# A hybrid encoder on one core: the attention core with scores over 128 rows and fewer, wider value products

## The chip, the cores and the metric

The kernel runs on one core of a Trainium2 chip. Its engines are PE (TensorE, matrix products, with its own weight loads), DVE (VectorE), ACT (ScalarE), POOL (GpSimd) and SP (SyncE, which here issues the DMAs). Matmul results land in PSUM, which has eight banks of 128 partitions by 512 float32 numbers; everything else stays in SBUF. The metric is the device time of one execution in microseconds, as a median of several runs.

## The reference

The program is an encoder of two layers on x of 512 positions and 1024 features, in float32. Cut to what matters, a layer computes:

```
h = rmsnorm(x); proj = h @ w_in        # 2304 columns: group A q, k, v and group B q, k, v
qa, ka, qb, kb = rope(rmsnorm per head of 64)
# group A: 8 query heads, 2 kv heads, dim 64, window of +-128, a sink logit per head
p = exp(s - m) / (sum exp(s - m) + exp(sink - m));   ya = p @ va
# group B: 4 heads, two score maps each (c = 0, 1), value dim 128
w = softmax(s[0]) - lam * softmax(s[1]);             yb = rmsnorm(w @ vb) * (1 - lam_init)
x = x + concat(ya, yb) @ w_out
h = rmsnorm(x); gate, val = split(h @ w_up)          # 2 x 2816 columns
x = x + (silu(dwconv3(gate)) * val) @ w_down
```

## The kernel before

**Precision.** A float32 operand is held as two float32r parts: high (the rounded value, written by ACT) and low (what is left, a subtraction on DVE). A product is the sum of three matmuls, high times high, high times low and low times high (`mm3`, L193 to L196). `split_out` (L245 to L247) makes the two parts of a result in PSUM. `emit_unit` does the same for the weights, which stream in over one DMA queue, three units ahead of their use.

**Stages of a layer.** Both the input projection of group A (`akv`, then `aq0`, `aq1`) and the feed-forward run as plain loops. Between them stands a weave of two tracks. One, `attend`, does group A in 8 units (a pair of query-head positions `ip` and a block of 128 queries `qb`) and then group B in 16 units (half, `qb`, head `j`). The other is a chain: the projections of B's first and second half (`proj_b`), the output projection in two passes, and the first half of its last part. `weave` takes the next step from the track that has used the smaller share of its budget (`ATT` 92.0 against 98.6), by the costs that the steps yield. `out_pass(0)` waits for group A's output, `out_pass(1)` for half 0 of B, B's half for its keys.

**Order.** The text of the program gives each instruction a priority, and a scheduler in the build puts the instructions of every engine into a fixed order; an instruction whose buffer is not free in its reckoning is passed by others. A tile of a pool goes into any free buffer of its tag. The matmuls on PE therefore do not stand in the order of the text.

**Queries and keys** (`qk_out`). A projected block of 128 positions is scaled, normed per head (the query's norm is kept apart in `rqa`, `rqb` and applied in the exponent), rotated by POOL and DVE, transposed by PE in the bank `tq`, and split into high and low, with two heads of 64 on the 128 partitions. The columns are permuted so that the two heads of one transposed block of A belong to kv heads 0 and 1.

**Scores.** `a_scores` (L399) and `b_scores` (L488) contract 64 rows: the heads, or the two maps c, lie in the two halves of the partitions. Each score tile takes three matmuls of 64 rows (L412 and L502). Then follow the row maximum on DVE, the exponent on ACT with the row's sum, and scaling or mixing on DVE.

**Values.** `a_values` (L445) transposes the probabilities of four heads in a key block into a bank of 512 columns, splits them, and multiplies them by A's values of both kv heads at once, three products of 512 columns a block. Of each kv head's product only the half of the partitions that belongs to it is kept. `b_values` (L520) transposes the mixed probabilities and adds up twelve products of 128 columns in half of the bank `acc`. `b_norm` (L544) norms, transposes and splits the result.

**Buffers.** `pair` (8) and `keep` (10) hold tiles of 128 x 2 x 512: split queries and keys, A's keys and values, B's values, the attention outputs, and in the feed-forward the hidden tiles `act`. `tmp` (7) holds scores and probabilities, `prob` (6) the transposed parts, `rp` (7) the projected blocks at work. Of PSUM, `mm` has 2 banks, `at` 4, `acc` 1 and `tq` 1.

Of the kernel before, what the change touches and what calls it, by code (L numbers as in the profile page):

```python
# [16 lines left out]
P = 128  # L17
S = 512
# [12 lines left out]
ATT = 92.0  # L31
AHEAD = 3
LAG = 2
RP = 7
# [9 lines left out]
def kernel(  # L44
# [23 lines left out]
    def pair(name):  # L68
        return sb.tile([P, 2, S], F32R, tag="pair", bufs=8, name=name)

    def keep(name):
        return sb.tile([P, 2, S], F32R, tag="keep", bufs=10, name=name)
# [4 lines left out]
    def prob(name):  # L77
        return sb.tile([P, S], F32R, tag="prob", bufs=6, name=name)

    def tmp(name, n=S):  # L80
        return sb.tile([P, n], F32, tag="tmp", bufs=7, name=name)
# [185 lines left out]
    for l in range(depth):  # L267
        lam_init = 0.8 - 0.6 * math.exp(-0.3 * l)
# [55 lines left out]
        def qk_out(bank, t, n, tab, dst, nm, rq):  # L324
            nh = n // HD
            nm = f"{nm}{l}_{t}"
            if n == P:
                raw = bank
            else:
                raw = rp(f"raw_{nm}")  # L330
                nc.scalar.activation(raw, bank[:, :n], AF.Copy, scale=r_tok[:, t:t + 1])
# [21 lines left out]
            nc.gpsimd.tensor_tensor(out=raw, in0=raw, in1=tb, op=ALU.add)  # L353
            tr = tq(f"tr_{nm}")
            nb = n // P
            for b in range(nb):
                nc.tensor.transpose(tr[:, b * P:(b + 1) * P], raw[:, b * P:(b + 1) * P], ident)
            split_out(dst[0][:, :, t * P:(t + 1) * P] if nb > 1 else dst[0][:, t * P:(t + 1) * P],
                      dst[1][:, :, t * P:(t + 1) * P] if nb > 1 else dst[1][:, t * P:(t + 1) * P],
                      tr[:, :n].rearrange("p (b q) -> p b q", q=P) if nb > 1 else tr[:, :n])  # L360
# [5 lines left out]

        # group A keys and values, then queries
        ka_t, va_t = keep(f"ka{l}"), keep(f"va{l}")
        ka = (ka_t[:, 0], ka_t[:, 1])
        va = (va_t[:, 0], va_t[:, 1])  # L370

        def akv_done(bank, t):
            raw = rp(f"raw_kv{l}_{t}")
            nc.scalar.activation(raw, bank[:, :CW], AF.Copy, scale=r_tok[:, t:t + 1])
            split_out(va[0][:, t * P:(t + 1) * P], va[1][:, t * P:(t + 1) * P], raw[:, P:])
            qk_out(raw[:, :P], t, P, tabs[1], ka, "ka", None)
# [4 lines left out]
        qa = [(pair(f"qah{l}_{i}"), pair(f"qal{l}_{i}")) for i in range(2)]  # L381

        def proj_a(i, alloc):
            yield from project(f"aq{i}", lambda bank, t: qk_out(
                bank, t, CW, tabs[0], qa[i], f"qa{i}", rqa[:, t, 2 * i:2 * i + 2, :].rearrange("p a b -> p (a b)")), alloc)
# [8 lines left out]
        ya = [(keep(f"yh{l}_{i}"), keep(f"yl{l}_{i}")) for i in range(2)]  # L394
# [4 lines left out]
        def a_scores(ip, qb):  # L399
# [3 lines left out]
            nm = f"a{l}_{ip}_{qb}"  # L403
            q, k = qa[ip], ka
            mx = small(f"mx_{nm}", 4)
            so = []
            for i in range(2):
                sc = [at(f"sc_{nm}_{i}_{g}") for g in range(2)]
                for j, (u, v) in enumerate(((0, 0), (0, 1), (1, 0))):
                    for g in range(2):  # L410
                        rs = slice(g * HD, (g + 1) * HD)
                        nc.tensor.matmul(sc[g][:, :n], lhsT=q[u][rs, i, qb * P:(qb + 1) * P],  # L412
                                         rhs=k[v][rs, kb0 * P:kb1 * P], start=j == 0, stop=j == 2)
                for g in range(2):
                    s = tmp(f"so_{nm}_{i}_{g}")
                    nc.vector.tensor_tensor_reduce(out=s[:, :n], in0=sc[g][:, :n], in1=mask_sb[:, m0:m0 + n],
                                                   op0=ALU.add, op1=ALU.max, scale=1.0, scalar=-3.0e38,
                                                   accum_out=mx[:, 2 * i + g:2 * i + g + 1])
                    so.append(s)
                yield 1.0  # L420
            by_g = lambda v: v.rearrange("p (g i) -> p i g", g=2)[:, 2 * ip:2 * ip + 2, :]
            pairs = lambda v: v.rearrange("p (i g) -> p i g", g=2)
            rq = rqa[:, qb, 2 * ip:2 * ip + 2, :]
            ngm = small(f"ng_{nm}", 4)
            nc.vector.tensor_tensor(out=pairs(mx), in0=pairs(mx), in1=rq, op=ALU.mult)
            nc.vector.scalar_tensor_tensor(out=pairs(ngm), in0=pairs(mx), scalar=-1.0, in1=by_g(nsink),
                                           op0=ALU.mult, op1=ALU.min)
            dn = small(f"dn_{nm}", 4)
            nc.vector.tensor_tensor(out=pairs(dn), in0=pairs(ngm), in1=by_g(sink), op=ALU.add)
# [3 lines left out]
            for i in range(4):  # L433
                nc.scalar.activation(so[i][:, :n], so[i][:, :n], AF.Exp, bias=ngm[:, i:i + 1],
                                     scale=rqa[:, qb, 2 * ip + i // 2, i % 2:i % 2 + 1],
# [52 lines left out]
        def b_scores(half, qb, j):  # L488
            h = 2 * half + j
            if j == 0:  # L490
                b_st[half, qb] = small(f"bl{l}_{half}_{qb}", 4)
# [304 lines left out]
```

## Time and profile before

| what | value |
|---|---|
| median of 3 runs | 1301.93 us (1301.84 to 1304.04) |
| span of the profiled execution | 1302.4 us |
| PE busy | 1270.6 us, 98% of the span |
| PE weight loads busy | 1056.6 us, 81% |
| DVE busy | 772.9 us, 59% |
| ACT busy | 557.5 us, 43% |
| POOL busy | 385.4 us, 30% |
| HBM read | 99.73 MB, 78 GB/s over the span |

| stage | from, to (us) |
|---|---|
| layer 0: first norm, projection of A | 0, 55 |
| layer 0: attention weave | 55, 285 |
| layer 0: end of output projection, norm, feed-forward | 285, 645 |
| layer 1: projection of A | 645, 691 |
| layer 1: attention weave | 691, 923 |
| layer 1: the rest | 923, 1302 |

The profile shows one execution. A line of groups names the program line, the engine, the operation, what it writes and reads, the shape and the count; behind the bar stand the busy time, the mean duration in ns, and the idle time ahead of it with what ended it. Lines in helpers (L194 to L196, L246, L247) serve many places, so the tile's name tells them apart. Matmuls overlap: the start of the next one, and not the duration, tells what one costs.

### The profile page before, as it was taken

How to read it: one execution, taken by the hardware profiler on the slowest of the kernel's cores; microseconds unless marked ns; L12 is line 12 of the kernel's file. 1: busy time of each engine (PE TensorE's matmuls, PEld its weight loads, DVE VectorE, ACT ScalarE, POOL GpSimd, SP SyncE). 2: the span in 40 equal slices, each digit the busy share in tenths (PEclk: the TensorE clock that was granted, in tenths of full speed). 3: DMA queues.
4: the chain of work that ended last, by engine and by line, in shares of the span. 5: the costliest groups of instructions: out<-in, count | busy, mean ns of one | idle time of the engine just before them, and what ended most of it. 6: DMA issues, size and time to landing. Idle time of an engine off the chain costs nothing. (4 is left out here: it accounts for less than half of the span.)

```text
span 1302.4 us, 17571 instructions
## 1 busy us (share of the span) xinstructions
PE 1270.6 (98%) x6744; PEld 1056.6 (81%) x6744; DVE 772.9 (59%) x1425; ACT 557.5 (43%) x1027; POOL 385.4 (30%) x446
## 2 busy tenths in 40 slices
PE   6999899999999999999999999999899999999998
PEld 6988788687888888888899878877788888888887
DVE  7678787767655324554466786767765543355532
ACT  4566555435433223333455656544443332233321
POOL 6847376114211000110156654741411110011100
PEclk8999999999999999999999999999999999999999
DMA  5211112113332233332331211111133322433232
GB/s 181 91 33 49 58 33 65 33 33 97 98 97 85 85 106 97 98 97 79 100 98 66 65 33 33 56 59 33 33 113 97 97 81 94 117 98 98 79 106 90
DMA packets 32628, 102.96 MB, mean 79 GB/s; under 512 B 3616, under 2 KB 4000, under 8 KB 32544
## 3 DMA queue, kind: packets, MB, share of 16 engines
q1 hardware_dynamic: 32544, 101.84, 25.6%
q8 instruction: 53, 0.87, 0.3%
q14 instruction: 31, 0.25, 0.1%
HBM read 99.73 MB, written 2.10 MB: 78 GB/s over the span
## 5 line engine op out<-in xcount | busy, mean ns | idle before, releaser
L181 ACT CAST wh<-wr 128x1024 fp32r<-128x1024 f32 (+3 forms) x210 | 197.7, 944 | 400.1 <-PE up L195 192.0
L195 PE MATMUL up<-nf_l,wh 128*128 128x512 f32 x704 | 275.3, 391 | 2.3 <-DVE nf_l L213 1.9
L196 PE MATMUL up<-nf_h,wl 128*128 128x512 f32 x704 | 274.5, 390 | 1.2 <-DVE wl L182 0.9
L194 PE MATMUL up<-nf_h,wh 128*128 128x512 f32 x704 | 272.9, 390 | 0.0
L182 DVE TENSOR_TENSOR wl<-wr,wh 128x1024 fp32r<-128x1024 f32 (+3 forms) x174 | 193.3, 1114 | 112.2 <-ACT wh L181 111.8
L702 POOL TENSOR_TENSOR cv<-cv,rb 128x512 f32<-128x512 f32 x44 | 57.8, 1316 | 521.5 <-ACT cv L701 521.5
L195 PEld LDWEIGHTS up<-nf_l,wh 128*128 128x128 f32 x704 | 132.1, 188 | 33.6 <-DVE nf_l L213 6.6
L196 PEld LDWEIGHTS up<-nf_h,wl 128*128 128x128 f32 x704 | 132.1, 188 | 29.7 <-DVE wl L182 2.9
L194 PEld LDWEIGHTS up<-nf_h,wh 128*128 128x128 f32 x704 | 132.2, 188 | 27.6
L195 PE MATMUL dn<-act,wh 128*128 128x512 f32 x352 | 138.5, 394 | 0.0
L196 PE MATMUL dn<-act,wl 128*128 128x512 f32 x352 | 138.4, 394 | 0.0
L194 PE MATMUL dn<-act,wh 128*128 128x512 f32 x352 | 137.9, 393 | 0.0
L182 POOL TENSOR_TENSOR wl<-wr,wh 128x1024 fp32r<-128x1024 f32 x36 | 87.1, 2421 | 89.4 <-ACT wh L181 89.4
L695 DVE TENSOR_TENSOR gp<-up,rb 128x512 f32<-128x512 f32 x44 | 30.3, 693 | 103.4 <-PE up L196 101.8
L703 DVE TENSOR_TENSOR cv<-cv,up 128x512 f32<-128x512 f32 x44 | 30.2, 687 | 82.6 <-POOL cv L702 73.0
L194 PEld LDWEIGHTS dn<-act,wh 128*128 128x128 f32 x352 | 66.0, 188 | 16.0
L195 PEld LDWEIGHTS dn<-act,wh 128*128 128x128 f32 x352 | 66.0, 187 | 15.7
L196 PEld LDWEIGHTS dn<-act,wl 128*128 128x128 f32 x352 | 66.0, 188 | 15.4
L716 DVE TENSOR_TENSOR x<-x,dn 128x512 f32<-128x512 f32 x32 | 22.0, 689 | 78.4 <-PE dn L196 78.4
L509 ACT ACTIVATE e_b<-sc_b,mx_b,rqb 128x512 f32<-128x512 f32 x64 | 49.2, 774 | 38.6 <-DVE mx_b L506 38.6
L701 ACT ACTIVATE cv<-cv 128x512 f32<-128x512 f32 x44 | 27.8, 632 | 76.4 <-DVE cv L700 76.3
L505 DVE TENSOR_REDUCE mx_b<-sc_b 128x1 f32<-128x512 f32 x64 | 42.0, 681 | 0.2
(211 smaller groups left out, 2713.7 us busy)
## 6 DMA issues: line engine op xcount, KB each, us to landing
wr<-w_up SPq DMA_DIRECT2D x88, 512.0 KB, 3.6
wr<-w_in SPq DMA_DIRECT2D x36, 512.0 KB, 3.7
wr<-w_down SPq DMA_DIRECT2D x32, 384.0 KB, 3.1
wr<-w_down SPq DMA_DIRECT2D x32, 320.0 KB, 2.9
wr<-w_out SPq DMA_DIRECT2D x16, 512.0 KB, 3.6
x<-xT SPq DMA_DIRECT2D x8, 256.0 KB, 5.3
outT<-x SPq DMA_DIRECT2D x8, 256.0 KB, 2.0
rows<-row_par SPq DMA_DIRECT2D x2, 260.0 KB, 5.0
```

Of the source, the lines that this page charges most:

```text
L181: nc.scalar.copy(hi[:, o], raw[:, o])
L182: eng.tensor_tensor(out=lo[:, o], in0=raw[:, o], in1=hi[:, o], op=ALU.subtract)
L194: nc.tensor.matmul(acc, lhsT=a[0], rhs=b[0], start=start, stop=False)
L195: nc.tensor.matmul(acc, lhsT=a[0], rhs=b[1], start=False, stop=False)
L196: nc.tensor.matmul(acc, lhsT=a[1], rhs=b[0], start=False, stop=stop)
L505: nc.vector.tensor_reduce(out=mx[:, c:c + 1], in_=sc[c], axis=AX, op=ALU.max)
L509: nc.scalar.activation(e[c], sc[c], AF.Exp, bias=mx[:, c:c + 1], scale=rq[:, c:c + 1], accum_out=lsum[:, 2 * j + c:2 * j + c + 1])
L695: nc.vector.tensor_tensor(out=g[:, 1:S + 1], in0=acc[0], in1=rb, op=ALU.mult)
L701: nc.scalar.activation(cv, cv, AF.Silu)
L702: nc.gpsimd.tensor_tensor(out=cv, in0=cv, in1=rb, op=ALU.mult)
L703: nc.vector.tensor_tensor(out=cv, in0=cv, in1=acc[1], op=ALU.mult)
L716: nc.vector.tensor_tensor(out=x_sb[d], in0=x_sb[d], in1=acc, op=ALU.add)
```

## The change

- **Keys** are written twice by POOL before the transpose (`k_twice`), so that each head's 64 rows stand on both halves of the partitions, once as high and once as low parts. Their tiles are of 128 x 4 x 512 (`kset`, 4 buffers).
- **Queries** stay as float32 rows until a block is needed. `q_stack`, now in the attention track, transposes it and stacks the high part of a head on one half of the partitions and the low part on the other.
- **Scores** then take two matmuls of 128 rows each: the stack against the doubled high keys, and against the doubled low keys. This adds the product of the two low parts.
- **Values of A**: a unit is now a kv head `g` and a block of queries, with its four heads. The stationary operand holds the kv head's high values in one half of the columns and its low values in the other; two products of 512 columns a block, one for each part of the probabilities. The two halves of the result are added afterwards, through a tile `rd`. Products follow the transposes one block behind.
- **Values of B**: the high parts of the probabilities meet high and low values side by side, 256 columns at once, and the low parts the high values, 128 columns. `acc` holds both results, and `b_norm` adds them.
- **Buffers**: one pool `blk` (10) and `kset` (4) stand in place of `pair` and `keep`; `rd` (2) and `qd` (3) are new; `tmp` has 6, `prob` 4, `rp` 4.
- **Weave**: budgets 73.0 and 107.0, and smaller costs for the attention's steps.

The diff, cut to its core:

```diff
-ATT = 92.0
+ATT = 73.0
+REST = 107.0
-RP = 7
+RP = 4
...
+    def blk(name, dtype=F32R):
+        return sb.tile([P, 2, S], dtype, tag="blk", bufs=10, name=name)
+    def kset(name):
+        return sb.tile([P, 4, S], F32R, tag="kk", bufs=4, name=name)
...
-            nc.gpsimd.tensor_tensor(out=raw, in0=raw, in1=tb, op=ALU.add)
+            if twice is None:
+                nc.gpsimd.tensor_tensor(out=raw, in0=raw, in1=tb, op=ALU.add)
+            else:
+                both = lambda v: v.rearrange("p (h d) -> p h d", d=HD).unsqueeze(2).broadcast_to([P, nh, 2, HD])
+                nc.gpsimd.tensor_tensor(out=twice.rearrange("p (h u d) -> p h u d", u=2, d=HD), in0=both(raw),
+                                        in1=both(tb), op=ALU.add)
+        def k_twice(bank, t, raw, tab, nm, hi, lo):
+            nh = raw.shape[1] // HD
+            tw = rd(f"tw_{nm}{l}_{t}")[:, :nh * P]
+            normed(bank, t, raw, tab, nm, None, tw)
+            tr = tq(f"tr_{nm}{l}_{t}")
+            for h in range(nh):
+                nc.tensor.transpose(tr[:, h * P:(h + 1) * P], tw[:, h * P:(h + 1) * P], ident)
+            split_out(hi[:, :, t * P:(t + 1) * P], lo[:, :, t * P:(t + 1) * P],
+                      tr[:, :nh * P].rearrange("p (h q) -> p h q", q=P))
+        def q_stack(pairs, nm):
+            tr = tq(f"tr_{nm}")
+            for i, q in enumerate(pairs):
+                nc.tensor.transpose(tr[:, i * P:(i + 1) * P], q, ident)
+            trv = tr[:, :2 * P].rearrange("p (i q) -> p i q", q=P)
+            st = qd(f"q_{nm}").rearrange("p (i c q) -> p i c q", c=2, q=P)
+            for c in range(2):
+                a, o = slice(c * HD, (c + 1) * HD), slice((1 - c) * HD, (2 - c) * HD)
+                nc.scalar.copy(st[a, :, c], trv[a])
+                nc.vector.tensor_tensor(out=st[o, :, c], in0=trv[a], in1=st[a, :, c], op=ALU.subtract)
+            return st
...
+            for i in range(4):
+                sc = at(f"sc_{nm}_{i}")
+                for u in range(2):
+                    nc.tensor.matmul(sc[:, :n], lhsT=a_q[qb][i // 2][:, i % 2, g], rhs=ka[:, 2 * u + g, kb0 * P:kb1 * P],
+                                     start=u == 0, stop=u == 1)
...
+            def product(b):
+                v = va[:, kb0 + b, 2 * g:2 * g + 2, :].rearrange("p x e -> p (x e)")
+                for u in range(2):
+                    nc.tensor.matmul(pv, lhsT=v, rhs=pb[b][u], start=b + u == 0, stop=b + u == nkb)
...
+            rs, ro = slice(g * HD, (g + 1) * HD), slice((1 - g) * HD, (2 - g) * HD)
+            y = rd(f"y_{nm}")
+            nc.scalar.copy(y[rs, :S], pv[ro])
+            nc.vector.tensor_tensor(out=y[rs, :S], in0=pv[rs], in1=y[rs, :S], op=ALU.add)
...
-            for i, (u, v) in enumerate(((0, 0), (0, 1), (1, 0))):
-                for c in range(2):
-                    rs = slice(c * HD, (c + 1) * HD)
-                    nc.tensor.matmul(sc[c], lhsT=q[u][rs, j, qb * P:(qb + 1) * P], rhs=k[v][rs, j, :],
-                                     start=i == 0, stop=i == 2)
+            for c in range(2):
+                for u in range(2):
+                    nc.tensor.matmul(sc[c], lhsT=b_st[half, qb, "q"][:, j, c], rhs=k[u][:, 2 * j + c, :],
+                                     start=u == 0, stop=u == 1)
...
+            for w, u in ((wh, 2), (wl, 1)):
+                for b in range(NT):
+                    v = vb[half, b // 2][:, b % 2, j, :u, :].rearrange("p u e -> p (u e)")
+                    nc.tensor.matmul(yb[:, 2 * j * P:(2 * j + u) * P], lhsT=w[:, b * P:(b + 1) * P], rhs=v,
+                                     start=u == 2 and b == 0, stop=u == 1 and b == NT - 1)
...
-            nc.scalar.copy(y, yb)
+            nc.scalar.copy(yv, yb[:, :, 0, :])
+            nc.vector.tensor_tensor(out=yv, in0=yb[:, :, 1, :], in1=yv, op=ALU.add)
...
-              (chain(proj_b(0), proj_b(1), out_pass(0, mm), out_pass(1, mm), out_tail()), 98.6))
+              (chain(proj_b(0), proj_b(1), out_pass(0, mm), out_pass(1, mm), out_tail()), REST))
...
-                a = (pair if f % 2 else keep)(f"act{l}_{f}")
+                if f - f0 < 10:
+                    a = blk(f"act{l}_{f}")
+                elif f - f0 == 10:
+                    last_act = kset(f"act{l}_{f}")
+                    a = last_act[:, 0:2]
+                else:
+                    a = last_act[:, 2:4]
```

More of the change, by code (lines that the diff above doesn't have):

```diff
@@ L77, in prob @@
     def prob(name):
[L78 removed]
+        return sb.tile([P, S], F32R, tag="prob", bufs=4, name=name)
     def tmp(name, n=S):
[L81 removed]
+        return sb.tile([P, n], F32, tag="tmp", bufs=6, name=name)
     def rp(name):
```

160 lines of the change are left out of this document (68 added, 92 removed).

## The prediction

> **What bounds the kernel now.** I read the page first, then the busy time of the engines stage by stage, the order of instructions on TensorE inside the stage that is changed, the groups of VectorE instructions, and the waits.
>
> ```profile
> PE 1270.6 (98%) x6744; PEld 1056.6 (81%) x6744; DVE 772.9 (59%) x1425; ACT 557.5 (43%) x1027; POOL 385.4 (30%) x446
> PE   6999899999999999999999999999899999999998
> DVE  7678787767655324554466786767765543355532
> PE 27%; DVE 0%; issue 0%
> ```
>
> TensorE (PE) is busy almost throughout, and what the chain of waits names is matmuls. But a matmul's busy time overlaps its successor's, so a busy PE says only that it is fed. VectorE (DVE) is busy in seven to eight tenths of slices 1 to 10 and 21 to 29: the two attention stages. The change lies almost wholly in these, and the stage table puts them at 55 to 285 us and 691 to 923 us:
>
> ```profile
> 120.00:130.00 10.00, 10.00 (x72) 8.72 (x71) 9.41 (x22) 7.31 (x19) 8.36 (x9) 1.00 0.18 53
> 130.00:140.00 10.00, 9.25 (x69) 8.15 (x68) 9.39 (x23) 3.64 (x10) 5.02 (x5) 1.00 0.18 54
> ...
> 55.00:285.00 230.00, 222.73 (x1418) 183.15 (x1418) 175.71 (x430) 125.56 (x300) 117.18 (x114) 0.99 0.15 48
> 691.00:923.00 232.00, 226.78 (x1464) 189.51 (x1462) 168.42 (x433) 127.50 (x301) 112.11 (x103) 0.99 0.16 47
> ```
>
> The columns after the length are PE, weight loads, DVE, ACT and POOL. PE fills 97% and 98% of the stages, DVE 76% and 73%. The first two rows are the densest DVE stretch that I found: 94% over 20 us, with PE at 96%. So PE bounds these stages, and DVE is the next engine, not far behind.
>
> **What a matmul costs here** is the distance from one start to the next. Three pieces of the PE's order of time (start, duration) give the prices:
>
> ```profile
> 148.53 0.28 PE L196 MATMUL pj_bq<-wh,na_l 128*128 128x256 f32 x1
> 148.66 0.28 PE L194 MATMUL pj_bq<-wh,na_h 128*128 128x256 f32 x1
> 148.86 0.49 PE L502 MATMUL sc_b<-bkh,bqh 64*128 64x512 f32 x1
> 149.20 0.39 PE L502 MATMUL sc_b<-bkl,bqh 64*128 64x512 f32 x1
> 149.43 0.39 PE L502 MATMUL sc_b<-bkh,bql 64*128 64x512 f32 x1
> 149.76 0.50 PE L194 MATMUL pv_a<-ph_a,va 128*128 128x512 f32 x1
> ...
> 863.31 0.50 PE L502 MATMUL sc_b<-bkl,bqh 64*128 64x512 f32 x2
> 863.64 0.40 PE L502 MATMUL sc_b<-bkh,bql 64*128 64x512 f32 x2
> 863.87 0.39 PE L502 MATMUL sc_b<-bkl,bqh 64*128 64x512 f32 x1
> 864.11 0.39 PE L502 MATMUL sc_b<-bkh,bql 64*128 64x512 f32 x1
> 864.43 0.33 PE L538 MATMUL yb<-vb,wth_b 128*128 128x128 f32 x1
> ```
>
> ```profile
> 255.28 0.27 PE L538 MATMUL yb<-vb,wth_b 128*128 128x128 f32 x1
> 255.39 0.28 PE L539 MATMUL yb<-vb,wth_b 128*128 128x128 f32 x1
> ...
> 125.19 0.33 PE L412 MATMUL sc_a<-ka,qah 64*128 64x384 f32 x1
> 125.36 0.33 PE L412 MATMUL sc_a<-ka,qal 64*128 64x384 f32 x1
> ...
> 126.19 0.39 PE L196 MATMUL pv_a<-ph_a,va 128*128 128x512 f32 x1
> 126.42 0.39 PE L194 MATMUL pv_a<-ph_a,va 128*128 128x512 f32 x1
> ...
> 119.09 0.60 PE L457 MATMUL pt_a<-ident,so_a 128*128 128x128 f32 x4
> 119.62 0.44 PE L412 MATMUL sc_a<-ka,qah 64*128 64x384 f32 x1
> ```
>
> 512 moving columns cost 0.23 us, 384 0.17, 256 about 0.12 (148.53 to 148.66), 128 0.11, a transpose 0.13. So halving a 256-column product into two of 128 nearly doubles its price. Three score matmuls of 64 rows take 0.90 us, not 3 x 0.23: 0.1 is lost when PE goes from 128 rows to 64, and 0.1 when it goes back. Where six of both halves stand together they take 1.12 us: two of them start together, so halves of the array do work side by side there.
>
> The Trainium skill, "TensorEngine Tiling (Array Packing)", under Overview and Key Properties, says that a contraction of at most 64 rows can run as two independent tiles, up to twice as fast, and that changing the tiling mode drains TensorE. That speaks against this change: by the first half of it six old score matmuls would cost 3 x 0.23 = 0.70 us and the four new ones 0.93, so the scores would get dearer, the gains of 25.5 and 18.8 us below would turn into losses of some 7 and 5, and of their sum about 5 us would be left. The trace agrees with the drain (0.1 us each way) and only in part with the overlap: most runs are threes of one half, because the order on PE has separated the halves.
>
> **The change on PE**, both layers together. The busy time of the two kinds of scores, as a tile's rows over the whole span (PE is the first column after the length; scores of B, then of A):
>
> ```profile
> 0.00:1302.40 1302.40, 54.85 (x192) 26.91 (x192) 42.02 (x64) 52.10 (x128) 0.99 0.26 79
> ...
> 0.00:1302.40 1302.40, 37.35 (x192) 23.12 (x192) 29.85 (x64) 0.99 0.26 79
> ```
>
> - Scores of B: 192 matmuls of 64 rows become 128 of 128 rows. 54.9 us goes to 128 x 0.23 = 29.4. Gain 25.5. Bounds: had all stood as sixes, 32 x (1.12 + 0.1) = 39 us, gain 9.6; all as threes, 64 x 1.0 = 64, gain 34.6. The row lies between and is taken.
> - Scores of A: 192 become 128, half of 384 and half of 256 columns: 37.4 goes to 64 x 0.17 + 64 x 0.12 = 18.6. Gain 18.8.
> - Values of A: 120 products of 512 columns become 80 (the stationary operand holds high and low values of one kv head, so one product does for two). Gain 40 x 0.23 = 9.2.
> - Values of B: 384 of 128 columns, 42.2 us, become 128 of 256 and 128 of 128: 15.4 + 14.1 = 29.5. Gain 12.7.
> - Transposes: keys are written twice side by side, so 32 more for B and 8 more for A: 40 x 0.13 = 5.2 lost. The query transposes move from the projection to the attention track, the same number.
>
> Sum on PE: 25.5 + 18.8 + 9.2 + 12.7 - 5.2 = 61.0 us, 30.5 a layer. The stages would last 199.5 and 201.5 us if PE alone set them.
>
> **The change on DVE and its neighbours.** Rows for the operations that multiply (busy, mean ns):
>
> ```profile
> L247 DVE TENSOR_TENSOR pl_a<-pt_a,ph_a 128x512 fp32r<-128x512 f32 x40 | 27.0, 684 | 6.1 <-ACT ph_a L246 6.0
> L247 DVE TENSOR_TENSOR yl<-pv_a,yh 64x256 fp32r<-64x256 f32 x32 | 13.4, 419 | 2.3 <-ACT yh L246 1.8
> L247 DVE TENSOR_TENSOR bkl<-tr_bk,bkh 128x256 fp32r<-128x256 f32 x16 | 6.6, 414 | 2.2 <-ACT bkh L246 2.2
> ...
> L246 ACT CAST ph_a<-pt_a 128x512 fp32r<-128x512 f32 x40 | 22.1, 586 | 14.3 <-PE pt_a L457 13.8
> L246 ACT CAST yh<-pv_a 64x256 fp32r<-64x256 f32 x32 | 11.7, 366 | 36.4 <-DVE yl L247 18.7 <-PE pv_a L196 17.5
> ...
> L702 POOL TENSOR_TENSOR cv<-cv,rb 128x512 f32<-128x512 f32 x44 | 57.8, 1316 | 521.5 <-ACT cv L701 521.5
> L353 POOL TENSOR_TENSOR raw_bk<-raw_bk,sq_bk 128x256 f32<-128x256 f32 x16 | 12.1, 758 | 1.0
> ```
>
> Fewer partitions buy nothing (64x256 costs what 128x256 does). Stacking a query block takes two subtractions of 64 partitions in place of one of 128: 32 stacks, 32 more at 0.42 = 13.4 us. B's key split widens from 256 to 512: 16 x 0.27 = 4.3; A's from 128 to 256, 8 x 0.13 = 1.0. A's two half sums must be added: 16 x 0.68 = 10.9. B's too: 16 x 0.42 = 6.7. Together 36.3 us, 18.2 a layer, none taken away. ACT gets 32 x 0.37 + 16 x 0.59 + 16 x 0.22 + 1 = 26 us, 13 a layer: 126 becomes 139 of some 215 us, so it hides behind PE and DVE; without that cover it would cost the 13. POOL's doubled key sum adds 16 x 0.56 = 9 us, and POOL is half idle. Half of the query subtractions, and the copies of A's sums, write other partitions than they read, which no row shows. Low bound the plain 0.42; high bound twice that, 6.7 us more a layer (16 shifted ones); I take the plain price, since partitions have not mattered in the rows.
>
> The smaller buffers (tmp 7 to 6, prob 6 to 4, rp 7 to 4, one pool of ten blocks) issue nothing, but take away depth. A unit of A holds four tmps from its masking to its last transpose; I price their loss at zero up to the rivals below. The feed-forward's hidden tiles move into the pool too, twelve tiles to twelve places; the second part's first tile needs one only after the first part's last down product, which stands ahead of it on PE anyway: nothing. No DMA moves, and the weight stream has the same order.
>
> **The sum.** After the change DVE has 175.7 + 18.2 = 193.9 and 168.4 + 18.2 = 186.6 us in stages for which PE needs 199.5 and 201.5. At the PE floor DVE would have to be 97% and 93% busy; the densest 20 us now are at 94%, and there PE already lost time. So part of the gain is lost to DVE. I take a DVE share of 0.90, between today's stage means (0.76, 0.73) and that densest stretch, nearer to the latter because a faster PE hands work over earlier: 193.9 / 0.90 = 215.4 and 186.6 / 0.90 = 207.3, that is 14.6 + 24.7 = 39.3 us less. The profiled execution has a span of 1302.4 us, 0.5 over the median of the runs; 1302.4 - 39.3 = **1263 us**. With 0.94 (PE's floor in layer 1) it is 1302 - 23.7 - 30.5 = 1248, with 0.85 1302 - 1.9 - 12.5 = 1288: the likeliest case's own range. All else (feed-forward, norms) is untouched.
>
> **Rivals.**
>
> 1. PE alone sets the time: 1302.4 - 61.0 = 1241 us. For it: PE is at 97% now, and DVE's idle time may be mere lack of input. Against it: 97% on DVE, over 200 us. Chance 0.22.
> 2. Slower: DVE's idle time is not slack but the wait for ACT in the middle of its order, and stays.
>
> ```profile
> DVE rl_b L513 <- ACT e_b L509: 12.3, 12, 1.7
> DVE ls_a L437 <- ACT so_a L434: 12.3, 7, 3.0
> ```
>
> In the first stage it waits 24.6 us at these two places (of 54 idle), in order, with the scaling and mixing of the probabilities queued behind, and PE's transposes waiting for those; six tmps leave less other work to fill it. It decides from a share of (193.9 + 186.6) / 462 = 0.82 downward; at 0.79 the stages last 482 us, so 1322. Against it: the 94% stretch has the same waits. Chance 0.12.
> 3. The block pool starves. While half 0 of B runs, A's values, queries and outputs, half 0's queries and values fill ten blocks; the freed three go to half 1's queries and values. The first norm of half 0 then has no block for its output until the first output pass has read A's. Behind it stand the one tq bank and the queries' stacks. Thirteen of 16 B units would run after that pass with little cover: DVE 13 x 5.3 + 9 = 78 us (5.3 = B's DVE work of 84.5 us a layer over 16) at 0.94, 83, after some 150 of PE work: 233 a stage. About 1304 us, no change. Against it: the weaving budgets (73 to 107) run the output pass earlier. Chance 0.12.
>
> **How the numbers follow.** Forecast 0.54, rivals 0.22, 0.12, 0.12. What this kernel's measurement can tell from no change is about 0.2%, 2.6 us. Faster: 0.54 + 0.22 and a third of rival 3, 0.80. Same: 0.06, the rest of rival 3's middle. Slower: rival 2 and the rest, 0.14. The range goes from 1238 to 1298: below the PE floor by little, up to a share of 0.83, with rival 2 and most of rival 3 left out.
>
> **What would show it.** Right: score rows of 128 rows 0.23 us apart with no 0.1 us steps around them, 128 B scores near 30 us; B's values in about 0.92 us per unit; the attention stages some 15 to 25 us shorter each, DVE at about 0.90 in them, PE with new gaps released by DVE; feed-forward unchanged at 360 us. PE near 97% in a shorter stage speaks for rival 1; a DVE share under 0.82 for 2; a stretch of output-projection matmuls with no B scores, then PE gaps, for 3. Wrong altogether would be score matmuls dearer than 0.23 us, or shifted writes at twice their price.

## The result and the profile after

The changed kernel takes **1405.16 us** (1404.07 to 1408.45) against 1302.99 us for the kernel before on the same chip, a ratio of **1.0764 [1.0725, 1.0804]**: 102 us slower, where 39 us less was forecast. The first part of its page:

```profile
PE 1261.6 (90%) x6488; PEld 1067.3 (76%) x6488; DVE 826.6 (59%) x1489; ACT 585.7 (42%) x1075; POOL 395.4 (28%) x446
...
PE   7977777787999999999998876797889999999998
...
DVE  7667675686755433555457777766866553345532
...
PEclk9988878898999999999999998897999999999999
```

The digits are tenths of 40 equal slices. PE has fallen to seven and eight tenths in most slices of the two attention stages (slices 1 to 9 and 21 to 29), DVE has not risen to its limit, and the granted clock of PE is down in many of the same slices. The stage table (start and end, length, then PE, weight loads, DVE, ACT and POOL, the clock, DMA) with the first weave, the middle part with the feed-forward, and the second weave:

```profile
59.00:346.00 287.00, 221.83 (x1295) 193.58 (x1295) 196.23 (x466) 138.85 (x319) 118.04 (x112) 0.85 0.12 36
346.00:707.00 361.00, 359.81 (x1575) 293.65 (x1574) 180.93 (x216) 130.71 (x169) 50.77 (x79) 1.00 0.31 95
754.00:1031.00 277.00, 218.98 (x1300) 189.28 (x1299) 197.44 (x458) 137.85 (x320) 107.65 (x96) 0.88 0.12 37
```

The middle part of the kernel before, in the same view:

```profile
285.00:645.00 360.00, 358.00 (x1583) 293.48 (x1584) 181.62 (x219) 129.37 (x168) 48.73 (x78) 1.00 0.30 92
```

It took 360 us there and 361 now. So the whole loss lies in the two weaves: 287 and 277 us, where 230 and 232 stood. DVE fills 196.23 / 287 = 68% and 71% of them, PE 77% and 79%. No engine is full.

How long did each group of the attention track run? Tile by tile the trace gives the first and the last start (here in layer 0); a group's length below is from its first scores to its last product of values. The rows of A and then of B, of the kernel before:

```profile
L412 PE MATMUL sc_a<-ka,qah x64: 272/339/446, 55.3 to 141.7; 64*128 64x256 f32 x32, 64*128 64x384 f32 x32
L196 PE MATMUL pv_a<-ph_a,va x20: 387/393/397, 75.7 to 169.4; 128*128 128x512 f32 x20
L502 PE MATMUL sc_b<-bkh,bqh x32: 393/493/501, 148.9 to 268.7; 64*128 64x512 f32 x32
L541 PE MATMUL yb<-vb,wtl_b x64: 223/274/328, 175.9 to 280.6; 128*128 128x128 f32 x64
```

And of the kernel after:

```profile
L445 PE MATMUL sc_a<-ka,q_a x64: 274/333/657, 59.1 to 170.9; 128*128 128x256 f32 x32, 128*128 128x384 f32 x32
L485 PE MATMUL pv_a<-pl_a,va x20: 390/405/794, 81.7 to 192.9; 128*128 128x512 f32 x20
L540 PE MATMUL sc_b<-bkh,q_b x32: 388/488/793, 176.0 to 316.2; 128*128 128x512 f32 x32
L575 PE MATMUL yb<-vb,wtl_b x64: 221/275/415, 199.3 to 333.5; 128*128 128x128 f32 x64
```

A went from 169.4 - 55.3 = 114.1 to 133.8 us, B from 131.7 to 157.5. Both groups run longer, by some 20 and 26 us, with fewer matmuls in them. (In layer 1 the same rows give 109.3 to 125.5 us for A and 129.0 to 154.2 for B.) Three places show where. PE in order of time (start, duration, what it waited for):

```profile
170.46 0.28 PE L203 MATMUL pj_bq<-wh,na_l 128*128 128x256 f32 x1
...
187.29 1.97 PE L490 MATMUL pt_a<-ident,so_a 128*128 128x128 f32 x8 [7.48 <-ACT e_b L547]
...
192.03 0.63 PE L540 MATMUL sc_b<-bkh,q_b 128*128 128x512 f32 x1
192.46 0.63 PE L540 MATMUL sc_b<-bkl,q_b 128*128 128x512 f32 x1
192.88 0.63 PE L485 MATMUL pv_a<-pl_a,va 128*128 128x512 f32 x1
...
195.67 0.28 PE L201 MATMUL pj_bq<-wh,na_h 128*128 128x256 f32 x1
...
200.88 0.39 PE L540 MATMUL sc_b<-bkh,q_b 128*128 128x512 f32 x1
201.11 0.39 PE L540 MATMUL sc_b<-bkl,q_b 128*128 128x512 f32 x1
...
209.37 0.56 PE L575 MATMUL yb<-vb,wtl_b 128*128 128x128 f32 x4
...
226.53 1.12 PE L373 MATMUL tr_bk<-ident,tw_bk 128*128 128x128 f32 x4 [9.61 <-POOL tw_bk L363]
...
231.19 0.38 PE L382 MATMUL tr_b<-ident,bq 128*128 128x128 f32 x2
...
237.01 0.39 PE L540 MATMUL sc_b<-bkh,q_b 128*128 128x512 f32 x1
...
243.49 0.63 PE L575 MATMUL yb<-vb,wth_b 128*128 128x256 f32 x4
```

And two rows of ACT in order of time:

```profile
193.55 0.84 ACT L337 ACTIVATE bq<-pj_bq,na_r 128x256 f32<-128x256 f32 x2 [0.86 <-PE pv_a L485]
...
254.77 0.48 ACT L611 ACTIVATE yh_b<-tr_yb,cols 128x256 fp32r<-128x256 f32 x1 [2.74 <-PE wo L202]
```

- **The other track stands still from 170 to 196 us.** The projection of half 1's queries stops at 170.46. Their result needs a block of the pool, and the copy into it starts at 193.55, right after the last product of A (192.88), the last reader of the block with A's values; at 195.67 the projection goes on. Until then PE has only the tail of A and B's first scores, and at 187.29 it has waited 7.48 us.
- **Half 1's keys come late**: PE waits 9.61 us for POOL's doubled keys at 226.53.
- **B pauses, and its outputs wait for the output projection.** There is no product of B's values from 209.4 to 243.5 us. The work that ends this pause follows the late keys: the next query stack, which uses the same `tq` bank, is transposed at 231.19, and its scores start at 237.01. The normed output `yh_b` of half 0 is written at 254.77, when the first output pass, which reads A's outputs, is nearly through. That is after the pause, so the wait of `yh_b` did not end it; what each of the two block waits costs by itself is not shown.

### The profile page after: what moved, and what is told of

It reads as the page before. It is cut to its first block, busy times and chain, and to the rows that moved or that the text cites. A ratio compares the mean times of both kernels' runs of the same rounds, so it can differ in the third digit from the quotient of the medians.

```text
span 1402.3 us, 17264 instructions
## 1 busy us (share of the span) xinstructions
PE 1261.6 (90%) x6488; PEld 1067.3 (76%) x6488; DVE 826.6 (59%) x1489; ACT 585.7 (42%) x1075; POOL 395.4 (28%) x446
## 5 line engine op out<-in xcount | busy, mean ns | idle before, releaser
L490 PE MATMUL pt_a<-ident,so_a 128*128 128x128 f32 x160 | 30.3, 329 | 35.9 <-DVE so_a L470 21.0
## 6 DMA issues: line engine op xcount, KB each, us to landing
x<-xT SPq DMA_DIRECT2D x8, 256.0 KB, 5.6
outT<-x SPq DMA_DIRECT2D x8, 256.0 KB, 2.0
```

The costliest lines, as they stand in the source:

```text
L490: nc.tensor.transpose(tr[:, i * P:(i + 1) * P], so[i][:, b * P:(b + 1) * P], ident)
```

## The experiments

Ratios are to runs of the kernel before on the same chip. Each version is put in order anew by the build, and the control c0 below, whose work is that of the changed kernel less six loads, came out at 1.0825 [1.075, 1.0899] against its 1.0764. So differences of less than about 8 us between two versions say nothing by themselves here. Some 5 us of c0's difference lie ahead of the first weave: its first scores of A start at 64.3 us, in the changed kernel at 59.1. All versions built on it start there at 62 to 64 us.

**A. Blocks and depth.** There is no room for more buffers beside the rest. To make it, the versions c0, c1, c2, c3 and d4 hold the eight residual tiles of x in two tiles, and d1, f3, f4, g3, h1 and h2 in one; only these are loaded, and every other instruction stays. The residual is then not the reference's, so these versions serve for their times alone.

```diff
# c0: the residual in two tiles, and nothing else
-    x_sb = [const.tile([P, S], F32, name=f"x{k}") for k in range(NK)]
+    x_one = [const.tile([P, S], F32, name=f"x{k}") for k in range(NK // 4)]
+    x_sb = [x_one[k // 4] for k in range(NK)]
# c1 = c0 and:
-        return sb.tile([P, 2, S], dtype, tag="blk", bufs=10, name=name)
+        return sb.tile([P, 2, S], dtype, tag="blk", bufs=12, name=name)
# c2 = c0 and: RP 4 -> 7, tmp 6 -> 7, prob 4 -> 6
# c3 = c1 and: RP 4 -> 7
# d1 = the residual in one tile, 12 blocks, tmp 7, prob 6 (RP stays 4)
```

> The changed kernel with the eight residual tiles of 2 KB held in two (x_one, so the residual is not the reference's; all instructions on it stay, six of its eight loads at the start fall away). It frees 12 KB and is the base of the next three. All theories: within 10 us of the changed kernel's 1405, the attention stages 285 and 274 us as there.

> The base with 12 blocks in the pool instead of 10. Theory 1, the pool starves: half 1's queries wait for group A's last values (copied at 193.55 us, 0.7 us after A's last product, though projected by 170), and the first norm of half 0 waits for the first output pass (copied at 254.8, ready at 216); two more blocks end both waits, and the stages fall by 25 us or more each, the total to 1355 or less. Theory 2, the depth of tmp, prob and rp: under 10 us gained. Theory 3, VectorE sets the pace: under 10 us.

> The base with rp 7, tmp 7, prob 6, as before the change, and the pool at 10. Theory 1: under 15 us gained, the two waits on blocks stay. Theory 2: 40 us or more gained, with the 9.9 us gap of TensorE at 217 us gone. Theory 3: under 10 us.

> The base with 12 blocks and rp 7 (tmp 6 and prob 4 stay). If theories 1 and 2 each hold in part: the sum of the two gains, the total near 1290 to 1320. Theory 1 alone: as with 12 blocks, within 10 us. If all waits on buffers end, the forecast's sum of 1263 is the floor that VectorE allows.

> The changed kernel with the residual's eight tiles held in one (so the residual is not the reference's), which makes room for 12 blocks, tmp 7 and prob 6; rp stays at 4. Read from the four runs before: 12 blocks ended the pause of group B (33.7 to 13.9 us) and deeper tmp, prob and rp shortened group A (137 to 121 us). If the two are separate and buffers are all that is wrong, A lasts about 121 and B about 130 us, the stage some 245 us, and the total 1330 or less. If something else holds group A (the one tq bank with the query stacks, or the pace of the other track), A stays above 130 us and the total above 1350.

| version | us | ratio to before |
|---|---|---|
| c0, control | 1415.22 | 1.0825 [1.0750, 1.0899] |
| c1, 12 blocks | 1373.09 | 1.0503 [1.0429, 1.0577] |
| c2, deep buffers | 1377.70 | 1.0538 [1.0465, 1.0611] |
| c3, 12 blocks and RP 7 | 1365.35 | 1.0444 [1.0373, 1.0514] |
| d1, 12 blocks, tmp 7, prob 6 | 1352.20 | 1.0326 [1.0302, 1.0351] |

Two more blocks take 42.1 us away, the depth of the small buffers 37.5, blocks with depth of tmp and prob 63.0. That is less than the first two together, but d1 also lacks c2's seven `rp` buffers; 12 blocks with all of c2's depth were not run, so whether the two gains add up is open. None of the four came near the 1290 to 1330 us that was expected if buffers were all that was wrong. In c1 B's rows of layer 0 read

```profile
L542 PE MATMUL sc_b<-bkh,q_b x32: 390/462/792, 185.0 to 301.6; 128*128 128x512 f32 x32
L577 PE MATMUL yb<-vb,wtl_b x64: 218/275/474, 214.0 to 316.2; 128*128 128x128 f32 x64
```

that is 131.2 us, the old length: with 12 blocks B's pause of 34 us is gone (the longest between two of its products is 14, as in the kernel before). A stays long there, 143.6 us (137.0 in c0):

```profile
L447 PE MATMUL sc_a<-ka,q_a x64: 274/332/668, 63.7 to 176.0; 128*128 128x256 f32 x32, 128*128 128x384 f32 x32
L487 PE MATMUL pv_a<-pl_a,va x20: 387/394/793, 86.2 to 207.3; 128*128 128x512 f32 x20
```

c2 shows the reverse. B stays at 157.4 us there, and A, 137.0 in c0, comes down to 120.7:

```profile
L487 PE MATMUL pv_a<-pl_a,va x20: 388/395/796, 84.8 to 183.1; 128*128 128x512 f32 x20
```

Its first scores start at 62.4 us. So the price of the pool of ten lies in B and that of the depth in A.

Depth alone, in the kernel before:

```diff
# e7 = before and
-RP = 7
+RP = 4
# tmp 7 -> 6, prob 6 -> 4
```

> The kernel before with tmp 6, prob 4 and rp 4 in place of 7, 6 and 7, nothing else. If depth costs group A as it does in the changed kernel (137 against 121 us): 10 us or more a layer, the total 1325 or more. If the depth matters only for the new order of work: under 8 us, 1310 or less.

1333.30 us, 1.0182 [1.0156, 1.0208]: the old kernel loses 24 us with the new kernel's depth and nothing else changed. Its engines run the same number of instructions. Again the loss is A's: 130.0 us for 114.1 in layer 0, 128.3 for 109.3 in layer 1, while B does not grow (129.0 and 126.0 us).

**B. Does TensorE set these stages?** e4 does one part of the change alone: B's values as 256 moving columns (12.7 us less on PE by the prediction's prices, one addition more on DVE). f1 leaves the third score matmul out (high keys with low queries), some 24 us of PE by the same prices. f2 leaves out the scaling of A's probabilities, 37 us of DVE and nothing of PE. h3 adds 72 products of 512 columns, whose result is overwritten (16.6 us by the same price).

```diff
# f1 = before and, for A; the same in B
-                for j, (u, v) in enumerate(((0, 0), (0, 1), (1, 0))):
+                for j, (u, v) in enumerate(((0, 0), (0, 1))):
# f2 = before and
-            for i in range(4):
-                nc.vector.tensor_scalar(out=so[i][:, :n], in0=so[i][:, :n], scalar1=rl[:, i:i + 1], scalar2=None,
-                                        op0=ALU.mult)
# h3 = before and, for A; in B ahead of wt with its keys
                 tr = at(f"pt_{nm}_{b}")
+                nc.tensor.matmul(tr, lhsT=va[0][:, (kb0 + b) * P:(kb0 + b + 1) * P], rhs=va[0], start=True, stop=True)
```

> The kernel before with one part of the change alone: B's values as 256 moving columns, the two half results added in the norm; buffers as before. TensorE's price list: 384 x 0.11 less 128 x 0.12 and 128 x 0.11 is 12.7 us less, all of it on the engine that bounds; VectorE gets 6.7 us that hide. So 1302 goes to about 1290 (ratio 0.990). If VectorE already sets the pace in the attention stages: no change or up to 7 us more.

> The kernel before with the third score matmul left out in both groups (high keys times low queries), which leaves its part out of the scores; nothing else is changed. It takes 128 matmuls from TensorE and nothing from any other engine. Theory P, TensorE's work sets the length of the attention stages: 64 x 0.23 + 32 x 0.17 + 32 x 0.12 = 24 us less, about 1281, ratio 0.98. Theory C, the attention track's chain from engine to engine sets the pace and TensorE is merely filled by the other track: under 8 us less, ratio 0.994 or more, as with B's values alone (1.0014).

> The kernel before with the scaling of group A's probabilities by the reciprocal of their sum left out (64 operations of VectorE, 37 us, four in a row in each unit between the exponents and the transposes), so group A's output is not normed. Theory P: no change beyond 4 us. Theory C: the chain of a unit of A gets 2.3 us shorter, 8 units a layer, so 10 to 35 us less in all, and TensorE's share of the stage goes up.

> The kernel before with one such product a bank: 72 x 0.23 = 16.6 us more TensorE work in stages where TensorE is already 97% busy at a clock of 0.99. If TensorE sets these stages, as the prediction had it: 1302 + 16.6, a ratio of 1.0127. If the tracks' chains set them and TensorE has slack that a busy share does not show: a ratio under 1.005.

| version | PE work by price | us | ratio to before |
|---|---|---|---|
| e4, B's values wide | 12.7 us less | 1309.21 | 1.0014 [0.9996, 1.0033] |
| f1, two score matmuls | 24 us less | 1295.56 | 0.9892 [0.9876, 0.9909] |
| f2, no scaling | the same | 1294.66 | 0.9888 [0.9874, 0.9903] |
| h3, filler | 16.6 us more | 1319.06 | 1.0083 [1.0053, 1.0113] |

Taking 12.7 us of PE work away bought nothing; 24 us bought 13.6; and 37 us of DVE work, off the engine that was called the next one and not the bound, bought 14.5. Adding 16.6 us cost 10.8 (6.9 to 14.8): between what the two theories expected (0.5% at most, or 1.27%), and so did f1's gain fall between its two.

f2 shows that PE's work alone does not set these stages, and e4 points the same way. f1 and h3 can't tell PE's work from the attention track's own length, for the score matmuls and the filler stand in that track as well as on PE. In f2 A got 10.7 and 6.2 us shorter in the two layers, the weaves only 4.5 and 2.2 (first scores to last values): B could not start as much earlier. My reading, not shown beyond this, is that PE with the other track and the attention track both stand near the limit, so that relief of one alone soon meets the other.

The stages of e4:

```profile
55.00:285.00 230.00, 218.09 (x1305) 177.63 (x1305) 176.34 (x427) 125.36 (x299) 117.01 (x113) 0.93 0.15 46
691.00:923.00 232.00, 223.27 (x1354) 182.45 (x1354) 170.85 (x425) 127.12 (x300) 114.33 (x105) 0.93 0.15 47
```

With less to do PE gets gaps (218.09 busy, 222.73 before) and its clock falls to 0.93 from 0.99. Over the whole run the products of B's values took 43.9 us of PE where they took 50.4, but the unchanged scores of B took 61.2 where they took 54.9 (single ones last 0.79 us). So a part of the saving came back as slower matmuls; what e4 would give at the full clock is not known. A and B run as long as ever in layer 0:

```profile
L412 PE MATMUL sc_a<-ka,qah x64: 272/339/443, 56.2 to 141.2; 64*128 64x256 f32 x32, 64*128 64x384 f32 x32
L196 PE MATMUL pv_a<-ph_a,va x20: 387/393/397, 75.1 to 169.8; 128*128 128x512 f32 x20
L502 PE MATMUL sc_b<-bkh,bqh x32: 393/497/793, 148.3 to 265.6; 64*128 64x512 f32 x32
L536 PE MATMUL yb<-vb,wtl_b x64: 222/275/473, 175.9 to 282.3; 128*128 128x128 f32 x64
```

113.6 us for A (114.1 before) and 134.0 for B (131.7).

**C. The 43 us that d1 still lacks.** In d1 B is at 136.1 us in layer 0 and A still at 132.6 (136.0 in layer 1), so most of it lies in A. Candidates: the weave's budgets, the sum of A's two halves, the place of the query stacks at the head of each block, A's scaling, and PE's lower clock. One more was not tried: d1 has four `rp` buffers, c2 with seven and ten blocks had A at 120.7.

```diff
# d4 = c3 and
-REST = 107.0
+REST = 85.0
# f3 = d1 with prob 5, qd 4, and the query stack of the next block made after the scores of this one
-            if g == 0:
-                a_q[qb] = [q_stack(...) for i in range(2)]
+                if (g, i) == (0, 3) and qb + 1 < NT:
+                    stack_a(qb + 1)
# f4 = d1 without the sum of A's halves: the split reads one half from PSUM
-            y = rd(f"y_{nm}")
-            nc.scalar.copy(y[rs, :S], pv[ro])
-            nc.vector.tensor_tensor(out=y[rs, :S], in0=pv[rs], in1=y[rs, :S], op=ALU.add)
# g3 = f3 without that sum and without the scaling (as f2)
# h1, h2 = d1 with two, four products ahead of each bank of transposes, overwritten by them
                 tr = at(f"pt_{nm}_{b}")
+                for _ in range(2):
+                    nc.tensor.matmul(tr, lhsT=va[:, kb0 + b, 2 * g:2 * g + 2, :]..., rhs=ka[:, g, :], start=True, stop=True)
```

> The kernel with 12 blocks and rp 7, and the other track's budget at 85 in place of 107, which holds the projections and the output passes back against the attention. Theory: at 107 the projections end at 181.5 us, before group A does at 200.2, and TensorE then has nothing to cover A's last units (a gap of 10.6 us at 183.7); held back, the projections last beyond A, the gap goes and the total falls by 10 to 25 us from 1365. If the gap comes from the chain of A's own work alone, under 5 us.

> The changed kernel with one residual tile, 12 blocks and tmp 7 (as in the run with 12 blocks and deeper buffers, but prob 5 and qd 4), and group A's query stacks for the next block made one unit ahead, after the fourth score, in place of right before the scores that use them. If the stack in the chain (transpose, two copies, two subtractions through the one tq bank) is what keeps group A at 133 to 136 us: A falls by 10 us or more a layer, the total to 1335 or less. If not: within 8 us of 1352.

> The kernel with one residual tile, 12 blocks, tmp 7 and prob 6, and the sum of group A's two halves left out: the high and low parts of the output are taken from one half of the result (so the low values' part is missing). It takes one copy of ScalarE (0.58 us) and one addition of VectorE (0.68) from each of the 8 units, and frees the one acc bank earlier. If this step in the chain holds A: 8 us or more a layer, the total 1336 or less. If it is hidden: under 5 us.

> The changed kernel with one residual tile, 12 blocks, tmp 7, prob 5, qd 4, the stacks made early, and without the sum of A's halves and without the scaling of A's probabilities (both left out of the result). Theory C, A's chain holds the stage: each step gives what it gave alone (4 and 10 us here, 14 us for the scaling in the kernel before), so 1320 to 1328, A near 110 us. If more than the chain of A is left, for instance group B or the pace of the tracks: A gets shorter and the stage does not, 1338 or more.

> The version with 12 blocks and deep buffers (d1, 1352 us; TensorE clock in its first stage 0.89) with two products of 512 columns put ahead of the transposes of every bank of probabilities; their result is overwritten, so nothing of the computation changes. 144 x 0.23 = 33 us more TensorE work, set where TensorE waits. If the lower clock in the gaps is what lengthens the chain (theory clock): the clock in the stages rises to over 0.93 and the time falls by 5 to 20 us, to 1332 to 1347. If the clock only follows the gaps (theory chain): the time is within 5 us of 1352, or up to 15 above, where a filler stands ahead of a transpose whose input was ready. If TensorE's work set the time: 1385.

> The same with four products a bank: 288 x 0.23 = 66 us more TensorE work, which brings TensorE's work in a stage from about 180 to about 213 of 258 us. Theory clock: the clock in the stages over 0.96, the time no higher than with two products. Theory chain: each filler that stands in the way adds to the chain, 1355 to 1385. If TensorE's work set the time: 1418.

| version | us | ratio to before |
|---|---|---|
| d4, budget 85 | 1411.50 | 1.0779 [1.0749, 1.0809] |
| f3, stacks early | 1348.18 | 1.0300 [1.0279, 1.0320] |
| f4, no sum | 1341.93 | 1.0252 [1.0231, 1.0272] |
| g3, stacks early, no sum, no scaling | 1316.39 | 1.0076 [1.0051, 1.0102] |
| h1, 33 us of filler | 1373.99 | 1.0498 [1.0461, 1.0535] |
| h2, 66 us of filler | 1374.58 | 1.0505 [1.0473, 1.0537] |

d4 is a plain miss: a smaller budget for the other track was to help by 10 to 25 us and cost 46; A ran 153.7 us in layer 0, where c3 had 136.9. The pace of the tracks matters, but not in the way I had thought.

The sum is worth 10.3 us, little more than two versions can be told apart by; the early stacks give 4.0, which is less. With the scaling gone as well, g3 comes to 1316.4, below its forecast of 1320 to 1328. The fair comparison is f2, the old kernel without the scaling. A's first and last rows in layer 0, f2 and then g3:

```profile
L412 PE MATMUL sc_a<-ka,qah x64: 271/379/447, 55.6 to 135.0; 64*128 64x256 f32 x32, 64*128 64x384 f32 x32
L196 PE MATMUL pv_a<-ph_a,va x20: 387/392/398, 75.1 to 159.0; 128*128 128x512 f32 x20
```

```profile
L450 PE MATMUL sc_a<-ka,q_a x64: 274/309/442, 63.1 to 144.9; 128*128 128x256 f32 x32, 128*128 128x384 f32 x32
L490 PE MATMUL pv_a<-pl_a,va x20: 390/394/796, 80.0 to 169.1; 128*128 128x512 f32 x20
```

That is 103.4 us and 106.0 (103.1 and 107.4 in layer 1): with the sum out and the stacks early, A is nearly as long as in the old kernel. So these two hold most of what d1's A had too much. Yet g3 stands at 1.0076 and f2 at 0.9888, 1.9% or some 25 us apart. Between their profiled executions, 21.7 us apart, 7.5 lie ahead of the first weave, 12.2 in the two weaves, 3.9 between them, and -1.9 behind. Of the 7.5, some 5 go with the residual's tiles, for c0 has them too; what makes the rest is not shown by any run. The stacks of B, B's own sum (L589), the keys through POOL and `rp` beside the deeper buffers were not tried alone.

Does PE's lower clock lengthen the chain? The first stages of d1, h1 and h2, over the same window of each:

```profile
59.00:335.00 276.00, 229.67 (x1379) 199.49 (x1378) 206.71 (x479) 148.87 (x340) 128.21 (x120) 0.89 0.14 44
```

```profile
59.00:335.00 276.00, 234.93 (x1417) 202.27 (x1418) 205.69 (x473) 143.64 (x330) 125.10 (x116) 0.93 0.15 44
```

```profile
59.00:335.00 276.00, 247.48 (x1494) 213.27 (x1493) 204.59 (x474) 143.72 (x331) 125.47 (x116) 0.95 0.14 44
```

The filler does raise the granted clock, 0.89 to 0.93 to 0.95, and the time goes up by 22 us, not down. The second 33 us of filler cost 0.6 us: PE has that much room there. That the first cost 22, more than the 15 that I had allowed, is not settled; it lengthens the way to the transposes that it stands ahead of, or another order came out. So a higher clock bought nothing here; as the filler has a price of its own, what the clock alone is worth is not shown.

**D. Is there a gain for the old kernel in this?** If A's chain and PE are both at the limit, easing both should pay. g1 moves two of A's four scalings to ACT, g2 adds B's wide values (e4) to it.

```diff
# g1 = before and
+                if i in (2, 3):
+                    nc.scalar.activation(so[i][:, :n], so[i][:, :n], AF.Copy, scale=rl[:, i:i + 1])
+                else:
```

> The kernel before with two of the four scalings of each unit of A done by ScalarE in place of VectorE; nothing is left out. VectorE loses 18.5 us, ScalarE gets 22, and the two pairs run side by side, so the chain of a unit is 1.2 us shorter. Theory C: 3 to 8 us less, ratio 0.994 to 0.998. Theory P: no change within 2 us.

> The same with B's values as 256 moving columns. If relief of VectorE lets TensorE's 12.7 us count in part: 5 to 12 us below 1309, and below the kernel with the scalings alone. If B's chain keeps its pace whatever TensorE does: no better than the scalings alone, since the wide values only add VectorE's 6.7 us.

1308.44 us, 1.0025 [1.0004, 1.0046], and 1307.33, 0.9991 [0.9972, 1.0010], beside 1307.54 for the kernel before: no gain, and g1 is a miss (3 to 8 us less was expected). In g1 A ran 114.4 and 110.6 us, as before the move (114.1 and 109.3): work moved from DVE to ACT stayed in the same chain and did not shorten it. No version that computes everything beats the kernel before.

## Why the prediction was wrong

**The step that failed first is "So PE bounds these stages", and with it the sum from engine totals** (PE's floor of 199.5 and 201.5 us, a DVE share of 0.90). The forecast went from a busy share of 97% to "less PE work, less time". e4 is the prediction's own edit of 12.7 us, and it was worth nothing; f2 took nothing from PE and gained 14.5 us. The attention track is a chain of products, maxima, exponents, scalings, transposes and splits on four engines, and it ran 114 us for A and 131.7 for B; the other track filled PE meanwhile. The two stages needed each group's length as a term, and the change lengthens A's chain by the stack and the sum.

**The second is "I price their loss at zero up to the rivals below"** for the smaller buffers. This is the largest term that was missing. c2 and e7 put a price on the depth: 37.5 us in the new kernel, 24 in the old. c1 puts 42.1 us on the blocks. d1 takes away 63 of the 107 us that the control c0 loses. This is shown. Of d1's other 43 us, the sum of A's halves and the place of the stacks make some 20, if the scaling is worth here the 14.5 that it gave in f2 (d1 to g3 is 35.8 us); the rest is open. So is where the forecast's gain went: no run had the new scores alone.

**Rival 3 named the right mechanism at the wrong price.** The wait that it described, `yh_b` for the first output pass, is in the trace. Half 1's queries wait as well, for a block that it counted as freed in time. It put 13 units of B behind the first output pass, in 83 us. (Its 233 us a stage come to 1306 us and not 1304; nothing hangs on that.) The last matmuls of that pass in layer 0:

```profile
L203 PE MATMUL wo<-yh,wl x32: 392/395/628, 228.3 to 256.0; 128*128 128x512 f32 x32
```

Four units were done when it ended at 256.0, and the other twelve ended at 333.5: 77.5 us. What it had wrong is the length of the first phase, "some 150 of PE work":

```profile
59.00:256.00 197.00, 152.82 (x934) 136.85 (x934) 134.46 (x318) 98.38 (x229) 109.03 (x104) 0.86 0.15 45
```

PE was busy for 152.8 us, in part at a lower clock, but the phase took 197, because PE was idle for the rest. It again priced a phase by PE's work alone, and so called a loss "no change".

**Rival 2 had the sign** and a threshold: DVE's share under 0.82. It came to 0.68 and 0.71. Its waits are longer, in the first stage of the kernel after:

```profile
DVE ls_a L466 <- ACT so_a L464: 18.3, 8, 3.0
...
DVE rl_b L551 <- ACT e_b L547: 14.8, 13, 1.7
```

33.1 us at its two places against 24.6. That is 8.5 of the 57 us by which the stage grew: too little to be the cause. Rival 1, PE alone, is out by PE's 77%.

**What was right, and a sign that failed.** Right are the matmul prices at full speed: 128-row scores stand 0.23 us apart (200.88 to 201.11) without a step around them. But the sign "128 B scores near 30 us" did not come. B's scores over the whole run, with PE first after the length:

```profile
0.00:1402.30 1402.30, 52.20 (x128) 26.90 (x128) 41.92 (x64) 52.12 (x128) 0.95 0.24 73
```

That is 52.2 us, where the kernel before has 54.9 in the same view. The forecast's gain of 25.5 was a row of busy time, in which each last matmul counts in full, less 128 starts 0.23 us apart. In the view of busy time a pair lasts 0.23 + 0.39 us (200.88, 201.11), so 64 pairs come to some 40 us even at full speed (an estimate from these two rows). Some ran slower: single ones of this tile last up to 0.79 us. The first stage's count fell from 1418 to 1295 matmuls, yet PE's busy time hardly did (222.73 to 221.83); part of them ran at half speed (192.03 to 192.88, 0.43 us apart).

The feed-forward stayed, 361 against 360 us. The prices of the new operations held too (groups by form with busy time and mean ns):

```profile
L388 DVE TENSOR_TENSOR q_b<-tr_b,q_b 64x256 fp32r<-64x256 f32 x32 | 13.5, 422 | 4.7 <-ACT q_b L387 3.8
L504 ACT COPY y_a<-pv_a 64x512 f32<-64x512 f32 x16 | 9.3, 580 | 7.5 <-PE pv_a L485 7.3
L505 DVE TENSOR_TENSOR y_a<-pv_a,y_a 64x512 f32<-64x512 f32 x16 | 11.0, 686 | 3.6 <-ACT y_a L504 3.4
L254 DVE TENSOR_TENSOR bkl<-tr_bk,bkh 128x512 fp32r<-128x512 f32 x16 | 11.0, 684 | 4.5 <-ACT bkh L253 4.4
L589 DVE TENSOR_TENSOR y_yb<-yb,y_yb 128x256 f32<-128x256 f32 x16 | 6.8, 423 | 1.8 <-ACT y_yb L588 1.6
```

0.42, 0.59 (ACT), 0.68, 0.68 and 0.42 us had been put in. By such rows the new operations add 36.8 us to DVE, where 36.3 was forecast. DVE's total rose by 53.7 us; among the rest are operations that the change does not touch and that took longer, and this was not followed up. Every price of a new operation held, and the sum missed by 142 us: what was missing is the order in which they wait for each other and for buffers.

## What to carry to other kernels

A busy share near 100% on an engine that two woven tracks feed says that the engine is fed, not that its work sets the time: give each track's chain a length from its first and last rows, and take out a little of the engine's work to see whether the time follows. Before pools are merged or made shallower, list who holds each buffer, until when, and whose last read frees it; here two blocks of twelve and three spare tiles were worth 63 us with the same computation. A phase with waits in it can't be priced by its work: 152.8 us of PE work took 197 us.

## What the runs showed of the hardware

- PE's granted clock fell to 0.85 and 0.88 in the two stages, where PE had gaps of up to 9.6 and 7.5 us. After the gap of 7.48 us that ends at 187.29, products of 512 columns start 0.43 us apart (192.03, 192.46, 192.88), at 200.88 0.23 apart. The Trainium skill, "TensorE: Matmul & The Clock Gate", Part 1, says that the clock drops to half after an idle window of about 3.4 us and comes back after a busy one; the trace agrees with the half speed. h1 and h2 raised the clock from 0.89 to 0.93 and 0.95 and gained nothing.
- An operation that writes other partitions than it reads costs the plain price. All subtractions of the query stack do (the prediction counted half), and take 0.422 us (L388) beside 0.419 for the same shape within its partitions before (`yl`); the copy of A's sum takes 0.580 us (L504), beside 0.586 for the split of `ph_a` within its partitions before.
- 16.6 us of PE work more (by price) in stages at 97% cost 10.8 us, and taking 12.7 out gave nothing: the two directions aren't mirror images.
